# Who normalises the attention weights, and when the convolution's taps run, in a two-layer hybrid kernel

## The chip, the core and the metric

The kernel runs on one core of a Trainium2 chip. The metric is device time in microseconds (us) of one execution. The core has five engines with in-order queues of their own: TensorE (PE; PEld is its weight load), VectorE (DVE), ScalarE (ACT), GpSimd (POOL) and SyncE (SP), which here only issues transfers.

## What is computed

The reference is a two-layer transformer over 512 latent tokens of width 1024, with 256 context tokens. The change touches layer 0 only, its mixer. One input projection feeds two branches, whose outputs are concatenated and multiplied by one output matrix:

```python
def attend(q, k, v):          # q (B,Q,H,QK), k (B,L,H,QK), v (B,L,H,V); 8 heads, 512 queries, 768 keys
    s = jnp.einsum('bqhd,bkhd->bhqk', q, k).astype(jnp.float32) * (QK_DIM ** -0.5)
    p = jax.nn.softmax(s, axis=-1).astype(v.dtype)
    return jnp.einsum('bhqk,bkhd->bqhd', p, v)
...
def conformer_conv(g, w_dw, b_dw, ln_g, ln_b):
    a, b = jnp.split(g, 2, axis=-1)
    z = a * jax.nn.sigmoid(b)
    z = lax.conv_general_dilated(z, w_dw[:, None, :], (1,), padding=[(15, 15)], ...) + b_dw   # 31 taps per channel
    return jax.nn.silu(layer_norm(z, ln_g, ln_b))
```

Queries, keys and values come from low-rank latents with norms and a rotary part. After the mixer, and again in layer 1 (a gated MLP over chunks), a mixture of 32 experts follows, each with its own weights from HBM.

## The kernel before

**The stages of layer 0's mixer**, with the stretch of the profiled execution that they take. Up to some 103 us: modulation, norms, the gated input of the convolution (`z`, 512 channels as four blocks of 128 partitions, 512 positions each). To 145 us: `latent(i)` (L1127), for two context blocks and four latent blocks of 128 tokens, each a product in three passes (`mm3`, the float32 weights split into a high and a low part). To 190 us: the keys and values of six token blocks (L1192) and the first two of the four blocks of queries (`query`, L1174). Then `attend` (L1235): 32 units of one head and one block of 128 queries. Then `Project.run` (L1478), the output projection, first with the attention's output, then with the convolution's.

**A unit of attention.** `scores(u)` (L1241): two products give 128 x 768 scores in PSUM; VectorE takes the maximum of each row (L1249) and scales it (L1250); ScalarE writes the exponentials to SBUF and sums them (L1252); VectorE takes the reciprocal of the sum (L1253) and multiplies the 768 columns by it, SBUF to SBUF (L1254). `values(u - 2)` (L1257), two units later: TensorE transposes the weights in six pieces (L1266), ScalarE copies four of them out of PSUM (L1269) and VectorE two (L1271); for every second unit TensorE multiplies them with the values of two heads (L1280), and the result is split into a high part by ScalarE and a low part by VectorE (`split`, L811). The loop at L1284 runs `scores(u)`, one tick of the queue `q`, `values(u - 2)`, at u of 3 and 11 a block of queries, and one step of `extra`, which computes modulation vectors for later (`ada`, eight 1 MB weight tiles for each of three groups, L826) and fetches.

**The convolution in the background.** `conv_steps` (L978) is a generator. Each of its first 31 steps adds one tap to all four channel blocks. Block 0 is always on VectorE, one instruction a tap (L991, both inputs and the output in SBUF). Block 1 is on VectorE as well in the first `NDVE` = 20 steps. Otherwise a block's tap is a scaling on ScalarE into a temporary (L996, a tile of the ring "w2" of 6) and an addition on GpSimd (L997). Then follow the sum over blocks, three empty steps, the mean, the variance, Sqrt, Silu and the split (L999 to L1029), 12 steps more.

**What sets the order.** `Later` (L40) holds the background work. Every `tick` adds `rate` to a credit, and each whole credit runs one step:

```python
        if self.bg:
            self.credit += self.rate
        while self.bg and self.credit >= 1:
            self.credit -= 1
            if next(self.bg[0], self) is self:
```

The rate is `RATE0` = 0.25 from L1115 on, `RATE1` = 1.0 in `attend`. There are 10 ticks in the latents (one for each context block, two for each latent block), 8 in the keys and first queries and 3 in the flush after them. So 5 steps (ticks 4, 8, 12, 16, 20) are done before the first unit, and one more with every unit. What is left after the loop is drained in the projection, by `conv()` (L1228). The taps' instructions on VectorE and ScalarE are kept in program order (`pin`); most others are placed on their queues by a planner that works out an order beforehand.

Of the kernel before, what the change touches and what calls it, by code (L numbers as in the profile page):

```python
# [12 lines left out]
AF = mybir.ActivationFunctionType  # L13
OP = mybir.AluOpType
# [781 lines left out]
def bank(k, name):  # L796
    return k.psum.tile([P, 512], F32, name=name, tag="ps")


def bank2(k, name):  # L800
    return k.psum.tile([P, 1024], F32, name=name, tag="pd", bufs=2)
# [176 lines left out]
def conv_steps(k, z, acc, ya):  # L978


    nc, pin = k.nc, k.tc.keep_in_program_order
    for m, j in enumerate([15] + [j for j in range(31) if j != 15]):
        lo, hi = max(0, 15 - j), min(512, 527 - j)
        for t in range(4):
            zz, d = z[:, t, lo + j - 15:hi + j - 15], acc[:, t, lo:hi]
            w = k.wdw[:, t, j:j + 1]
            if t == 0 or (t == 1 and m < NDVE):
                if m == 0:
                    pin(nc.vector.tensor_scalar(d, zz, w, k.bdw[:, t:t + 1], op0=OP.mult, op1=OP.add))
                else:  # L990
                    pin(nc.vector.scalar_tensor_tensor(d, zz, w, d, op0=OP.mult, op1=OP.add))  # L991
            elif m == 0:
                pin(nc.scalar.activation(d, zz, AF.Identity, bias=k.bdw[:, t:t + 1], scale=w))
            else:
                tp = k.work.tile([P, 512], F32, name="ctp", tag="w2", bufs=NW2)[:, 0:hi - lo]
                pin(nc.scalar.activation(tp, zz, AF.Copy, scale=w))  # L996
                nc.gpsimd.tensor_tensor(d, d, tp, op=OP.add)  # L997
        yield
# [33 lines left out]
def attention_mixer(k, x, ctx, extra, proj):  # L1032

    nc, q = k.nc, k.q
# [129 lines left out]

    for i in (4, 5, 0, 1, 2, 3):
        latent(i)

    wuk = load_parts(k, [k.w_ukv], 2, 1024, "wuk", nc.gpsimd)
    wuq = [load_parts(k, [k.w_uq[b]], 3, 384, "wuq", nc.gpsimd) for b in range(2)]
# [53 lines left out]
    ya = Parts(k, 4, 512, "yc")  # L1223
    back.append(ya)
    attend(k, qx, kx, kc, vt, y, extra, query, proj)
    q.rate = RATE2

# [7 lines left out]
def attend(k, qx, kx, kc, vt, y, extra, query, proj):  # L1235

    nc, q = k.nc, k.q
    units = [(hp, i, e) for i in range(4) for hp in range(4) for e in range(2)]
    held, PTs = {}, {}

    def scores(u):  # L1241
        hp, i, e = units[u]
        h = 2 * hp + e
        ps = bank2(k, "ps_s")
        a = qx[h // 4][0:QK, h % 4, i * P:(i + 1) * P]
        nc.tensor.matmul(ps[:, 0:512], a, kx[h // 4][0:QK, h % 4], start=True, stop=True)
        nc.tensor.matmul(ps[:, 512:768], a, kc[0:QK, h], start=True, stop=True)
        mx = k.small.tile([P, 4], F32, name="mx4", tag="mx4", bufs=4)
        nc.vector.tensor_reduce(mx[:, 0:1], ps[:, 0:768], axis=AX.X, op=OP.max)  # L1249
        nc.vector.tensor_scalar(mx[:, 1:2], mx[:, 0:1], -SCALE, None, op0=OP.mult)  # L1250
        pr = k.work.tile([P, 768], F32, name="pr", tag="t3", bufs=4)
        nc.scalar.activation(pr, ps[:, 0:768], AF.Exp, bias=mx[:, 1:2], scale=SCALE, accum_out=mx[:, 2:3])  # L1252
        nc.vector.reciprocal(mx[:, 3:4], mx[:, 2:3])  # L1253
        nc.vector.tensor_scalar(pr, pr, mx[:, 3:4], None, op0=OP.mult)  # L1254
        held[u] = pr

    def values(u):  # L1257
        hp, i, e = units[u]
        pr = held.pop(u)
        if e == 0:  # L1260
            PTs[0] = k.work.tile([P, 2, 6, P], F32, name="PT", tag="PT", bufs=2)
        PT = PTs[0]
        for a, b in ((0, 4), (4, 6)):
            pt = bank(k, "ps_pT")
            for c in range(a, b):
                nc.tensor.transpose(pt[:, (c - a) * P:(c - a + 1) * P], pr[:, c * P:(c + 1) * P], k.ident)  # L1266
            src = pt[:, 0:(b - a) * P].rearrange("p (c t) -> p c t", c=b - a)
            if a == 0:
                nc.scalar.copy(PT[:, e, a:b], src)  # L1269
            else:  # L1270
                nc.vector.tensor_copy(PT[:, e, a:b], src)  # L1271
        if e == 0:
            return

        def pv():
            po = bank(k, "ps_pv")
            for c in range(6):
                for e in range(2):
                    v = vt[hp // 2][:, c, 128 * (hp % 2) + 64 * e:128 * (hp % 2) + 64 * e + 64]
                    nc.tensor.matmul(po[64 * e:64 * e + 64, 0:P], v, PT[:, e, c, :], start=(c == 0), stop=(c == 5))  # L1280
            split(k, y(0, hp, i * P, i * P + P), y(1, hp, i * P, i * P + P), po[:, 0:P])
        q.push(YL, pv)

    for u in range(len(units) + 2):  # L1284
        if u < len(units):
            scores(u)
        q.tick()
        if u >= 2:
            values(u - 2)
        if u in QK1:  # L1290
            query(len(QK0) + QK1.index(u), False)
        if u == 26:
            proj.fetch()
        next(extra, None)
    q.flush()
# [296 lines left out]
QK1 = [3, 11]  # L1592
PRE0 = [4, 2, 1, 0]
PRE1 = [0, 0, 0, 0, 0, 2, 2, 0]
NDVE = 20
RATE0, RATE1 = 0.25, 1.0


def body(tc, nc, x, ctx, cc, w_ada, w_ada0, b_ada, norm1, norm2, w_ab, w_glu, w_lat, w_uq, w_ukv, ab_w_out, c_w_in, c_b_in, c_lng, c_lnb, c_wsT,
# [272 lines left out]
```

## Time and profile before

| | |
|---|---|
| median of 3 runs | 1419.5 us (1416.41 to 1420.37) |
| the profiled execution's own time | 1422.08 us |
| its span, first to last instruction | 1420.3 us |
| TensorE busy, share of the span | 1223.8 us, 86% |
| VectorE | 743.0 us, 52% |
| ScalarE | 514.3 us, 36% |
| GpSimd | 288.6 us, 20% |
| mean granted TensorE clock | 0.949 of full speed |

A profile is of one execution. Busy time of an engine is the time in which it worked on an instruction; matmuls are pipelined, and their ends are modelled, so that TensorE's share is not its distance from its peak. An idle engine costs nothing unless another waits for it. The shares are means over stages with different limits, and the stage that the change touches takes about a fifth of the span.

### The profile page before, as it was taken

Reading aid. Unit: us, or ns where it says so; the run is one execution under the profiler, and the core shown is the slowest. Engines: PE = TensorE matmul, PEld = TensorE weight load, DVE = VectorE, ACT = ScalarE, POOL = GpSimd, SP = SyncE. Lnnn points to the kernel's source line nnn. Section 1 sums busy time; section 2 is a strip of 40 time slices with the busy share of each in tenths; the row PEclk is TensorE's granted clock in tenths of the full one; section 3 lists DMA queues with packets and bytes.
Section 4 is the critical chain, followed back from the end, with each engine's and each line's share of the span. In section 5 each row is a group of like instructions: output and inputs, shape, how many; then the busy total and the mean of one; then the engine's idle time right before and its main releaser. Section 6 shows DMA issues by size and latency. Waiting matters only on the chain. (4 is left out here: it accounts for less than half of the span.)

```text
span 1420.3 us, 19799 instructions
## 1 busy us (share of the span) xinstructions
PE 1223.8 (86%) x6894; PEld 793.5 (56%) x6894; DVE 743.0 (52%) x1598; ACT 514.3 (36%) x1235; POOL 288.6 (20%) x270
## 2 busy tenths in 40 slices
PE   5999878899996989989969999999995787777775
PEld 2678654455673444444458898997873333333333
DVE  2334778889567556564684456667346411111116
ACT  3244554476444434333352233335224312211111
POOL 0033455587002011121230001221002100000000
PEclk9999989899997999999989999999997999999998
DMA  9401044726847799989856364453367699988883
GB/s 359 160 29 47 18 155 149 296 72 245 318 157 260 282 365 413 413 347 381 366 179 221 105 231 135 159 172 131 148 237 261 241 365 358 366 342 326 347 325 124
DMA packets 59298, 341.13 MB, mean 240 GB/s; under 512 B 9817, under 2 KB 10073, under 8 KB 24370
## 3 DMA queue, kind: packets, MB, share of 16 engines
q1 hardware_dynamic: 50834, 314.68, 57.1%
q0 software_dynamic: 8224, 23.61, 5.0%
q8 instruction: 106, 1.74, 0.5%
q14 instruction: 134, 1.10, 0.2%
HBM read 321.96 MB, written 21.80 MB: 242 GB/s over the span
## 5 line engine op out<-in xcount | busy, mean ns | idle before, releaser
L357 PE MATMUL mps<-w,xT 128*64 128x512 f32 x1024 | 250.2, 640 | 44.5 <-issue 30.5
L357 PEld LDWEIGHTS mps<-w,xT 128*64 128x64 f32 x1024 | 100.2, 147 | 188.9 <-issue 183.4
L806 PE MATMUL ps_c<-wch,hxh 128*128 128x256 f32 x512 | 147.7, 289 | 2.0 <-ACT hxh L812 2.0
L808 PE MATMUL ps_c<-wch,hxl 128*128 128x256 f32 x512 | 146.0, 286 | 1.5 <-DVE rm_m L98 0.9
L807 PE MATMUL ps_c<-wcl,hxh 128*128 128x256 f32 x512 | 146.2, 286 | 0.0
L363 DVE TENSOR_TENSOR mix<-mix,mps 128x256 f32<-128x256 f32 x32 | 13.5, 421 | 235.0 <-ACT mix L362 235.0
L430 PE MATMUL mps<-w,mix 128*64 128x512 f32 x512 | 116.9, 598 | 8.4 <-ACT mix L371 6.6
L362 ACT ACTIVATE mix<-mps 128x256 f32<-128x256 f32 x32 | 12.3, 384 | 275.1 <-PE mps L357 275.1
L997 POOL TENSOR_TENSOR acc<-acc,ctp 128x497 f32<-128x497 f32 (+14 forms) x71 | 103.1, 1481 | 29.4 <-ACT ctp L996 29.4
L806 PEld LDWEIGHTS ps_c<-wch,hxh 128*128 128x128 f32 x512 | 99.1, 194 | 7.8 <-issue 4.2
L808 PEld LDWEIGHTS ps_c<-wch,hxl 128*128 128x128 f32 x512 | 99.0, 194 | 4.5 <-issue 1.7
L807 PEld LDWEIGHTS ps_c<-wcl,hxh 128*128 128x128 f32 x512 | 99.2, 194 | 4.2 <-issue 3.4
L411 POOL TENSOR_TENSOR X<-X,tmp 128x512 f32<-128x512 f32 x32 | 41.2, 1287 | 203.8 <-ACT tmp L410 180.4
L430 PEld LDWEIGHTS mps<-w,mix 128*64 128x64 f32 x512 | 35.1, 136 | 71.5 <-issue 54.3
L400 PE MATMUL mps<-oy,ooh 128*128 128x512 f32 x272 | 72.7, 408 | 1.7 <-ACTq L729 1.7
L413 DVE TENSOR_TENSOR X<-X,mps 128x512 f32<-128x512 f32 x101 | 64.6, 683 | 5.8 <-PE mps L400 4.9
L806 PE MATMUL ps_o<-woh,yTh 128*128 128x512 f32 x160 | 63.9, 402 | 2.9 <-DVE res L1538 1.7
L807 PE MATMUL ps_o<-wol,yTh 128*128 128x512 f32 x160 | 63.6, 397 | 0.0
L808 PE MATMUL ps_o<-woh,yTl 128*128 128x512 f32 x160 | 62.9, 394 | 0.0
L400 PEld LDWEIGHTS mps<-oy,ooh 128*128 128x128 f32 x272 | 48.5, 189 | 24.9 <-issue 12.1
L812 POOL TENSOR_TENSOR vs<-v,vs 128x512 fp32r<-128x512 f32 x16 | 23.0, 1440 | 182.1 <-ACT vs L812 174.7
L991 DVE SCALAR_TENSOR_TENSOR acc<-z,cl,acc 128x508 f32<-128x508 f32 (+14 forms) x49 | 58.8, 1223 | 0.0
(429 smaller groups left out, 2408.4 us busy)
## 6 DMA issues: line engine op xcount, KB each, us to landing
w<-in_w_gu_dram SPq DMA_DIRECT2D x128, 1024.0 KB
w<-in_w_down_dram SPq DMA_DIRECT2D x64, 1024.0 KB
wada<-in_w_ada_dram SPq DMA_DIRECT2D x48, 1024.0 KB
wc<-in_c_w_in_dram SPq DMA_DIRECT2D x16, 1024.0 KB
wo<-in_c_w_out_dram SPq DMA_DIRECT2D x8, 1024.0 KB
X<-in_x_dram SPq DMA_DIRECT2D x4, 1024.0 KB
wo<-in_ab_w_out_dram SPq DMA_DIRECT2D x4, 1024.0 KB
yd<-zero SPq DMA_DIRECT2D x4, 1024.0 KB
```

The costliest lines, as they stand in the source:

```text
L357: k.nc.tensor.matmul(m.pg[64 * h:64 * h + 64, :], m.xT[:, c, 64 * h:64 * h + 64], st.gu(p, h, c), start=(c == 0), stop=(c == 7))
L363: k.nc.vector.tensor_tensor(m.h, m.sg, m.pg[:, 256:512], op=OP.mult)
L400: k.nc.tensor.matmul(po, self.oh[:, i * P:i * P + P], y[:, 512 * n:512 * n + 512], start=start and y is self.y[0], stop=stop and y is self ...
L411: k.nc.gpsimd.tensor_tensor(X[i][:, c], X[i][:, c], m.tmp, op=OP.add)
L413: k.nc.vector.tensor_tensor(X[i][:, c], X[i][:, c], po, op=OP.add)
L430: nc.tensor.matmul(m.py[n][64 * h:64 * h + 64, :], m.hT[:, f, 64 * h:64 * h + 64], st.dn(p, h, f)[:, 512 * n:512 * n + 512], start=(f == 0 ...
L806: k.nc.tensor.matmul(out, lh, rh, start=start, stop=False)
L807: k.nc.tensor.matmul(out, lh, rl, start=False, stop=False)
L808: k.nc.tensor.matmul(out, ll, rh, start=False, stop=stop)
L812: for i in (k.nc.scalar.copy(hi, src), (eng or k.nc.vector).tensor_tensor(lo, src, hi.bitcast(F32), op=OP.subtract)):
L991: pin(nc.vector.scalar_tensor_tensor(d, zz, w, d, op0=OP.mult, op1=OP.add))
L997: nc.gpsimd.tensor_tensor(d, d, tp, op=OP.add)
```

## The change

The normalisation L1254 leaves VectorE: `normal(u)` does it on ScalarE, as a copy with a scale for each row, issued after the unit's tick and before `values(u - 2)`. In the convolution, block 1 stays on VectorE in all 31 steps, not in 20. The rate is 0.75 while the latents are computed, 0.25 with the keys and first queries (`RATE01`), and 1.0 in the attention loop as before.

```diff
--- before.py
+++ after.py
@@ -984,7 +984,7 @@
         for t in range(4):
             zz, d = z[:, t, lo + j - 15:hi + j - 15], acc[:, t, lo:hi]
             w = k.wdw[:, t, j:j + 1]
-            if t == 0 or (t == 1 and m < NDVE):
+            if t < 2:
                 if m == 0:
                     pin(nc.vector.tensor_scalar(d, zz, w, k.bdw[:, t:t + 1], op0=OP.mult, op1=OP.add))
                 else:
@@ -1164,6 +1164,7 @@
 
     for i in (4, 5, 0, 1, 2, 3):
         latent(i)
+    q.rate = RATE01
 
     wuk = load_parts(k, [k.w_ukv], 2, 1024, "wuk", nc.gpsimd)
     wuq = [load_parts(k, [k.w_uq[b]], 3, 384, "wuq", nc.gpsimd) for b in range(2)]
@@ -1251,12 +1252,15 @@
         pr = k.work.tile([P, 768], F32, name="pr", tag="t3", bufs=4)
         nc.scalar.activation(pr, ps[:, 0:768], AF.Exp, bias=mx[:, 1:2], scale=SCALE, accum_out=mx[:, 2:3])
         nc.vector.reciprocal(mx[:, 3:4], mx[:, 2:3])
-        nc.vector.tensor_scalar(pr, pr, mx[:, 3:4], None, op0=OP.mult)
-        held[u] = pr
+        held[u] = pr, mx
+
+    def normal(u):
+        pr, mx = held[u]
+        nc.scalar.activation(pr, pr, AF.Copy, scale=mx[:, 3:4])
 
     def values(u):
         hp, i, e = units[u]
-        pr = held.pop(u)
+        pr, _ = held.pop(u)
         if e == 0:
             PTs[0] = k.work.tile([P, 2, 6, P], F32, name="PT", tag="PT", bufs=2)
         PT = PTs[0]
@@ -1285,6 +1289,8 @@
         if u < len(units):
             scores(u)
         q.tick()
+        if u < len(units):
+            normal(u)
         if u >= 2:
             values(u - 2)
         if u in QK1:
@@ -1592,8 +1598,7 @@
 QK1 = [3, 11]
 PRE0 = [4, 2, 1, 0]
 PRE1 = [0, 0, 0, 0, 0, 2, 2, 0]
-NDVE = 20
-RATE0, RATE1 = 0.25, 1.0
+RATE0, RATE01, RATE1 = 0.75, 0.25, 1.0
 
 
 def body(tc, nc, x, ctx, cc, w_ada, w_ada0, b_ada, norm1, norm2, w_ab, w_glu, w_lat, w_uq, w_ukv, ab_w_out, c_w_in, c_b_in, c_lng, c_lnb, c_wsT,
```

## Rows read from the trace of the kernel before

**Rows 1.** Windows by stage: length, busy us (instructions) of each engine, TensorE's clock, DMA.

```profile
103.00:145.00 42.00, 38.67 (x253) 36.83 (x252) 17.43 (x50) 16.96 (x53) 17.60 (x31) 1.00 0.15 47
145.00:190.00 45.00, 35.35 (x175) 29.55 (x174) 34.59 (x90) 21.23 (x56) 17.01 (x19) 0.92 0.25 100
190.00:341.00 151.00, 130.06 (x806) 70.44 (x805) 131.14 (x232) 87.34 (x167) 105.51 (x81) 0.91 0.43 159
341.00:366.00 25.00, 23.83 (x182) 15.55 (x183) 19.14 (x38) 12.93 (x26) 9.38 (x8) 1.00 0.92 337
366.00:380.00 14.00, 11.62 (x55) 8.92 (x55) 7.99 (x10) 6.87 (x10) 0.00 (x0) 0.97 1.02 422
```

**Rows 2.** Groups, 190 to 341 us: shapes, count | busy us, mean ns | idle before.

```profile
L991 DVE SCALAR_TENSOR_TENSOR acc<-z,cl,acc 128x508 f32<-128x508 f32 (+14 forms) x42 | 51.9, 1259 | 0.0
L1249 DVE TENSOR_REDUCE mx<-ps_s 128x1 f32<-128x768 f32 x28 | 26.5, 947 | 2.1 <-PE ps_s L1247 2.1
L1254 DVE TENSOR_SCALAR pr<-pr,mx 128x768 f32<-128x768 f32 x27 | 26.5, 981 | 0.5
L1271 DVE COPY PT<-ps_pT 128x256 f32<-128x256 f32 x25 | 10.3, 413 | 8.3 <-PE ps_pT L1266 8.2
L1253 DVE RECIPROCAL mx<-mx 128x1 f32<-128x1 f32 x27 | 4.2, 154 | 4.2 <-ACT pr L1252 4.1
...
L996 ACT ACTIVATE ctp<-z,cl 128x501 f32<-128x501 f32 (+14 forms) x65 | 42.2, 710 | 1.0 <-DVE ada_sb L843 1.0
L1252 ACT ACTIVATE pr<-ps_s,mx 128x768 f32<-128x768 f32 x27 | 24.2, 899 | 25.4 <-DVE mx L1250 23.7 <-PE ps_pT L1266 1.6
...
L997 POOL TENSOR_TENSOR acc<-acc,ctp 128x501 f32<-128x501 f32 (+14 forms) x65 | 94.2, 1480 | 23.1 <-ACT ctp L996 23.1
```

**Rows 3.** Waits from 190 to 341 us: total, times, longest.

```profile
ACT pr L1252 <- DVE mx L1250: 23.7, 13, 5.2
...
PE ps_pT L1266 <- DVE yTl L812: 8.2, 4, 2.8
...
PE ps_pT L1266 <- DVE PT L1271: 5.2, 4, 1.8
```

**Rows 4.** One line's instructions: shortest, median and longest in ns.

```profile
L991 DVE SCALAR_TENSOR_TENSOR acc<-z,cl,acc x49: 677/1206/2770, 131.8 to 337.4; 128x508 f32<-128x508 f32 x4, 128x509 f32<-128x509 f32 x4, 128x510 f32<-128x510 f32 x4, 128x511 f32<-128x511 f32 x4
...
L1254 DVE TENSOR_SCALAR pr<-pr,mx x32: 603/797/1717, 193.9 to 362.0; 128x768 f32<-128x768 f32 x32
...
L997 POOL TENSOR_TENSOR acc<-acc,ctp x71: 1062/1552/2456, 136.8 to 340.2; 128x497 f32<-128x497 f32 x5, 128x498 f32<-128x498 f32 x5, 128x499 f32<-128x499 f32 x5, 128x500 f32<-128x500 f32 x5
```

**Rows 5.** Timeline of TensorE from 340.8 us: start, duration, instructions.

```profile
340.82 1.12 PE L1246 MATMUL ps_s<-kx,qx 96*128 96x512 f32 x2
...
344.57 1.06 PE L826 MATMUL ps_ada<-wada,sc 128*32 128x512 f32 x8
345.57 1.12 PE L1246 MATMUL ps_s<-kx,qx 96*128 96x512 f32 x2
...
346.96 1.02 PE L1006 MATMUL ps_m<-csum,avg 128*128 128x512 f32 x2
347.83 0.82 PE L1266 MATMUL ps_pT<-ct,pr 128*128 128x128 f32 x6
...
349.57 0.70 PE L1246 MATMUL ps_s<-kx,qx 96*128 96x512 f32 x1
```

**Rows 6.** Timeline of GpSimd, 129 to 160 us, and a wait from 103 to 190.

```profile
129.32 4.74 POOL L812 TENSOR_TENSOR wukl<-wuk,wukh 128x1024 fp32r<-128x1024 f32 x2 [4.87 <-ACT wukh L812]
...
146.93 2.94 POOL L812 TENSOR_TENSOR wuql<-wuq,wuqh 128x384 fp32r<-128x384 f32 x3 [1.23 <-ACT wuqh L812]
151.49 0.62 POOL L1207 TENSOR_TENSOR kt<-krr,hrs 128x256 f32<-128x256 f32 x1 [1.62 <-DVE hrs L102]
155.02 3.48 POOL L997 TENSOR_TENSOR acc<-acc,ctp 128x498 f32<-128x498 f32 x2 [2.91 <-ACT ctp L996]
...
PE ps_hd L970 <- POOL kt L1207: 6.5, 3, 3.4
```

**Rows 7.** Timeline of TensorE in the output projection: idle time in brackets.

```profile
378.63 0.50 PE L806 MATMUL ps_o<-woh,ych 128*128 128x512 f32 x1 [2.38 <-ACT ych L812]
```

## The prediction, made before the change was run

> **What bounds the kernel now.** I read the busy times by stage first. The change touches the stretch from the latent projections to the output projection, so only that is cut into stages [rows 1]. Before 145 us TensorE is busy 38.7 of 42 us: the projections are TensorE-bound, and VectorE, ScalarE and GpSimd each work less than half of the time. From 145 to 190 (keys, values, first queries) TensorE drops to 35.4 of 45. From 190 to 341, attention with the convolution's taps woven in, VectorE is busy 131.1 of 151 us, 87%. TensorE shows 130.1, but at a granted clock of 0.91; at full clock that is 130.1 x 0.91 = 118 us. From 341 to 366, with the taps gone, TensorE is busy 23.8 of 25 at clock 1.00.
>
> The groups of 190 to 341 [rows 2] show what fills VectorE: 42 taps 51.9 us, the row maxima 26.5, the normalisation 26.5, the copies of transposed weights 10.3. The reader should see two means: a tap takes 1259 ns and a normalisation 981, though the shortest of each is 677 and 603 [rows 4]. GpSimd's additions likewise take 1480 on average against a shortest 1062. All three read and write SBUF, and as I read it they stretch each other when VectorE and GpSimd meet. The waits [rows 3] show the consequence: the transposes of the weights wait for VectorE (8.2 and 5.2 us), for the small copies that sit behind a pair of taps, and ScalarE's exponentials wait 23.7 us for the scaled maximum. So this stage is set by VectorE's queue and its meeting with GpSimd.
>
> What TensorE alone would need is seen after 341: two units with one product of attention weights and values, from 340.82 to 349.57, less 0.87 for a product of the convolution's mean, so 7.88 us a pair or 3.94 a unit, 1.00 of it modulation work [rows 5]. The stage holds 27 exponentials, so 27 units, in 151 us: 5.6 us each.
>
> **The change, part by part.** *Normalisation moved.* 27 instructions of 0.98 us leave VectorE in this stage, 26.5 us. On ScalarE the same 768 columns are bounded by the exponential over 768 columns, 0.90 us, and, from below, by the 500-column scaling of the taps, 0.71 us [rows 2]; I take 0.90, the same width, so 24 us more for ScalarE. ScalarE waits with it for the reciprocal; behind it on its queue stand the copy of unit u-2's transposes and the next exponential, which TensorE and VectorE wait for. Between exponential and normalisation lie the tap's two scalings, 1.4 us, which should cover the reciprocal. *Half of the convolution on VectorE.* In steps 20 to 30 one channel block goes from ScalarE and GpSimd to VectorE: 11 scalings and 11 additions less, 11 taps more. *Taps earlier.* A step costs one credit. The latents give 10 ticks, the keys and the flush 11. At 0.25 throughout, 5 steps are done when attention begins; at 0.75 and then 0.25 it is 7 in the latents and 3 after them, 10 in all. The steps among the keys stay on the ticks that they had. In the attention loop the taps end with unit 20 instead of 25, and the whole chain behind them (mean, variance, swish) now ends on the tick of unit 32, before the output projection.
>
> Attention stage, VectorE: it had 42 taps and 27 normalisations; it gets 42 taps (21 steps of two) and none, while GpSimd's additions fall from 65 to 42. VectorE falls to 131 - 26.5 = 105 us, and lower if the taps shrink with GpSimd's load. ScalarE: 87.3 + 24 - 23 x 0.71 = 95. GpSimd: 105.5 - 23 x 1.48 = 71. TensorE then leads. Its work lies between 27 x 3.94 = 106 (no query projections in it) and 118; I take 114, above the middle for the projections. No engine reaches 100% in a loop of in-order queues that wait for each other; the leading one had 87% before, and I take the same for TensorE: 114 / 0.87 = 131 us, against 151, so **-20 us**. Bounds: TensorE without a gap at the middle, 112, gives -39; VectorE's queue staying what sets the pace gives about 0.
>
> *Tail.* TensorE waits 2.38 us for the convolution's output in the output projection [rows 7]. With the chain ended inside the loop this goes: **-2.4 us** (0 to -4; next in line is the next weight's split). Its Sqrt and Silu table loads now fall among the last exponentials; if the order puts Sqrt between two of them, two reloads come in, on a ScalarE that is idle 12 of the 25 us there [rows 1].
>
> *Latents and keys.* Five steps come in: 10 taps on VectorE (0.68 to 1.26 us each, 7 to 13 us), 10 scalings on ScalarE (7 us), 10 additions on GpSimd (1.06 to 1.48, 11 to 15). Before 145 they are costed at nothing: TensorE's own 38.7 us covers them, with VectorE at 17.4 and GpSimd at 17.6 of 42 [rows 1]. What is not covered is the last of them, on the last latent's last tick, just ahead of the first keys. GpSimd also splits the key and query weights there (4.74 us for one pair) and multiplies the rotary keys at 151.49, and TensorE already waits 6.5 us for that product [rows 6]. A pair of additions before it costs 2 to 3.5 us. Bounds: 0, if the queue is empty by then, as it was from 149.9, and +5 with a second pair behind; I take **+3**.
>
> No transfer is added. Faster units, at 114 / 0.87 / 27 = 4.9 us or at best 4, ask for the modulation weights sooner: 1 MB in 4 us is 262 GB/s, against the 422 GB/s that the queue moves from 366 to 380 [rows 1]. The expert weights are issued as slots come free, so they move with TensorE.
>
> Sum: -20 - 2.4 + 3 = -19.4. The profiled execution took 1422.1 us (span 1420.3 and 1.8 around it), which gives 1402.7; it lies 2.6 over the median of the runs shown, so the median to expect is **1400 us**.
>
> **Rivals.** *The meeting of VectorE and GpSimd still sets the pace.* Two taps and two additions remain in every one of 21 units, and only the normalisation has gone. For it: the taps' mean of 1259 against 677 is the larger share of the stretch. Against it: GpSimd's additions fall by a third. The units with taps stay at 5.6 us, five of them become units without (5 x (5.6 - 3.94) = 8 us), tail -2.4, keys +3: 1419.5 - 7.4 = 1412. The Trainium skill, "SBUF — State Buffer", Who interferes with whom, gives this mechanism as an exclusive lock that a VectorE instruction with two SBUF inputs and a GpSimd instruction that reads SBUF take in turn. By that rule the taps alone keep the lock busy, and 1412 is the time; the rows bear out the stretch, not that it decides.
>
> *ScalarE's queue becomes the bound (the other side).* Place: the normalisation of unit u, which waits for VectorE's reciprocal. If the order leaves the reciprocal behind the previous step's taps (a pair takes 2.5 us at the mean), ScalarE stands, and the next exponential and the copy behind it with it. Price: 2 us in each of 21 units is 42 us, against the 19.4 of the sum: 1419.5 - 19.4 + 42 = 1442. It decides from 1.0 us a unit on. For it: ScalarE at 95 of 131 us, with VectorE's answer needed in each unit. Against it: the scalings stand between, and before, the reciprocals waited 4.2 us in all for exponentials [rows 2]. The Trainium skill, "ScalarE: Activation LUTs", Rules for kernel authors, speaks against the change outright: multiplications belong on VectorE. By that rule each move loses 0.3 us (0.90 against 0.60), some 10 us; the trace agrees only for the shortest instruction, the mean of 0.98 is above 0.90.
>
> *The early taps delay the keys in full.* All ten additions end up ahead of the weights' splits: 10 x 1.06 = 11 us more on the path, so 1400 + 11 - 3 = 1408.
>
> **How the numbers follow.** My forecast 0.68, the lasting lock 0.15, ScalarE's queue 0.09, the early taps 0.08. Within 0.3%, or 4.3 us, is about what a measurement of this kernel can tell from no change. Faster by more: 0.66 of the forecast, 0.10 of the lock case (1412 lies not far past the line at 1415.2), 0.07 of the early taps, 0.83. Slower by more: ScalarE's queue 0.09 and 0.01 of the lock case, 0.10. The rest is 0.07. The range runs from -38 (TensorE nearly without a gap, 1381) to 1417, which takes in the lock case and the delayed keys; outside are ScalarE's queue and the edges.
>
> **What would show it.** Right: from the first score to the last, some 20 us less; TensorE busy over 85% of the loop with a granted clock nearer 1; VectorE under 85%; the waits of the transposes for VectorE below half; the taps' mean near 1.0 us; no wait for the convolution's output in the projection. Wrong: units with taps still at 5.6 us; ScalarE waiting for the reciprocal by tens of us; a gap before the first keys' transposes of over 5 us.

## The result, and the profile after

The change made the kernel slower: 1426.5 us median (1418.8 to 1435.1, 20 runs) against 1416.5 (1410.4 to 1428.5, 20 runs), a ratio of 1.0066, 95% interval 1.0047 to 1.0084. Forecast were 1400 us, at most 1417. The profiled execution after has a span of 1422.6 us, 2.1 under its median less the 1.8 around it; that of before lies 5.6 over its own. So the two traces differ by only 2.3 us where the medians differ by 10.0: medians say how much, and the traces say where.

The windows ahead of the attention come first, from the first product of the latents to the last one and from there to the first score: two rows of before, then two of after. Then come the 27 units of after from the first score on. The columns are those of [rows 1], and the last row sums the two windows above it.

```profile
101.78:144.58 42.80, 39.47 (x258) 37.66 (x257) 18.12 (x51) 16.92 (x52) 18.40 (x31) 1.00 0.13 42
144.58:188.56 43.98, 34.34 (x172) 29.02 (x171) 33.15 (x86) 21.27 (x56) 17.43 (x20) 0.92 0.27 106
...
100.61:154.33 53.72, 42.56 (x259) 40.40 (x257) 29.32 (x59) 21.43 (x60) 30.06 (x40) 0.94 0.11 36
154.33:204.70 50.37, 36.78 (x172) 30.94 (x172) 37.41 (x88) 22.14 (x58) 19.68 (x21) 0.86 0.22 89
...
204.70:239.70 35.00, 27.34 (x146) 14.53 (x146) 24.16 (x57) 21.52 (x37) 17.82 (x20) 0.90 0.19 66
239.70:340.80 101.10, 92.44 (x640) 51.48 (x638) 81.07 (x153) 75.75 (x137) 65.87 (x47) 1.00 0.62 237
sum 136.10, PE 119.78 PEld 66.01 DVE 105.22 ACT 97.26 POOL 83.69; mean PE 59.89 PEld 33.00 DVE 52.61 ACT 48.63 POOL 41.84
```

The latents take 10.9 us more and the keys and first queries 6.4 more, 17.3 in all. Of this 11.8 us are idle time of TensorE (7.8 in the latents, 4.0 behind them), and 5.5 are the same products at a lower clock (0.94 for 1.00, then 0.86 for 0.92). The first score comes at 204.7 us instead of 188.6. The same 27 units that took 149.2 us before (first exponential 192.7, the 28th 341.9) take 136.1. The gain is there, and it was spent before the attention began.

The rows of the attention's groups in those 136 us, of after, answer to [rows 2] (line numbers are one to five higher; L1259 is the moved normalisation):

```profile
L997 POOL TENSOR_TENSOR acc<-acc,ctp 128x505 f32<-128x505 f32 (+14 forms) x44 | 63.6, 1470 | 25.6 <-ACT ctp L996 25.6
L991 DVE SCALAR_TENSOR_TENSOR acc<-z,cl,acc 128x505 f32<-128x505 f32 (+14 forms) x44 | 49.5, 1158 | 0.0
...
L1259 ACT ACTIVATE pr<-pr,mx 128x768 f32<-128x768 f32 x26 | 24.3, 934 | 4.3 <-DVE mx L1254 4.1
L1253 ACT ACTIVATE pr<-ps_s,mx 128x768 f32<-128x768 f32 x27 | 24.2, 897 | 14.3 <-DVE mx L1251 9.5 <-PE ps_pT L1270 1.9 <-DVE a2c L854 1.7
```

The normalisation on ScalarE takes 0.93 us and waits 4.1 us in all for the reciprocal; the exponentials wait 9.5 us for the scaled maximum, not 23.7 [rows 3].

What TensorE waited for from 100 to 210 us, of after (total, times, longest):

```profile
PE ps_latT L1160 <- DVE lt L1155: 14.5, 5, 4.7
PE ps_hd L970 <- POOL kt L1208: 6.7, 3, 3.6
```

The second row is as before [rows 6]. The first was, in the kernel before:

```profile
PE ps_latT L1160 <- DVE lt L1155: 3.0, 4, 1.6
```

TensorE stands at the transposes of the latents' normalised rows. The timeline of after around the longest of these waits, ScalarE, GpSimd, VectorE and TensorE in turn:

```profile
129.33 0.49 ACT L1140 ACTIVATE jkl<-ps_lat 128x384 bf16<-128x384 f32 x1 [4.35 <-PE ps_lat L808]
129.72 0.19 ACT L1140 ACTIVATION_READ_ACCUMULATOR jkl<-ps_lat 128x1 f32 x1
129.81 0.70 ACT L996 ACTIVATE ctp<-z,cl 128x499 f32<-128x499 f32 x1
130.42 0.28 ACT L97 ACTIVATE rm_y<-lst,eps 128x2 f32<-128x2 f32 x1
...
130.59 2.44 POOL L997 TENSOR_TENSOR acc<-acc,ctp 128x499 f32<-128x499 f32 x2 [3.30 <-ACT ctp L996]
132.99 2.34 POOL L812 TENSOR_TENSOR wukl<-wuk,wukh 128x1024 fp32r<-128x1024 f32 x1
...
130.73 0.17 DVE L99 RECIPROCAL rm_y<-rm_y 128x2 f32<-128x2 f32 x1 [0.61 <-ACT rm_y L97]
130.93 0.93 DVE L100 TENSOR_TENSOR rm_a<-rm_y 128x2 f32<-128x2 f32 x1
131.89 1.17 DVE L101 SCALAR_TENSOR_TENSOR rm_a<-rm_a,rm_m 128x2 f32<-128x2 f32 x1
133.09 2.26 DVE L102 SCALAR_TENSOR_TENSOR lst<-rm_a,rm_y 128x2 f32<-128x2 f32 x1
135.39 1.01 DVE L1155 SCALAR_TENSOR_TENSOR lt<-ps_lat,lst,gains 128x256 f32<-128x256 f32 x2
...
130.93 0.29 PE L808 MATMUL ps_lat<-wih,hxl 128*128 128x288 f32 x1
135.93 1.49 PE L1160 MATMUL ps_latT<-ct,lt 128*128 128x128 f32 x5 [4.71 <-DVE lt L1155]
...
137.77 0.52 PE L807 MATMUL ps_lat<-wil,hxh 128*128 128x384 f32 x1
138.09 0.52 PE L808 MATMUL ps_lat<-wih,hxl 128*128 128x384 f32 x1
...
139.54 0.33 PE L808 MATMUL ps_lat<-wih,hxl 128*128 128x384 f32 x1
```

The same chain in the kernel before, one latent at the same place, ScalarE, VectorE and TensorE:

```profile
127.78 0.19 ACT L1140 ACTIVATION_READ_ACCUMULATOR jkl<-ps_lat 128x1 f32 x1
...
128.54 0.16 DVE L100 TENSOR_TENSOR rm_a<-rm_y 128x2 f32<-128x2 f32 x1
128.73 0.16 DVE L101 SCALAR_TENSOR_TENSOR rm_a<-rm_a,rm_m 128x2 f32<-128x2 f32 x1
128.93 0.16 DVE L102 SCALAR_TENSOR_TENSOR lst<-rm_a,rm_y 128x2 f32<-128x2 f32 x1
129.13 1.01 DVE L1155 SCALAR_TENSOR_TENSOR lt<-ps_lat,lst,gains 128x256 f32<-128x256 f32 x2
...
129.45 0.29 PE L808 MATMUL ps_lat<-wih,hxl 128*128 128x288 f32 x1
...
130.28 0.52 PE L1160 MATMUL ps_latT<-ct,lt 128*128 128x128 f32 x3 [0.18 <-DVE lt L1155]
```

Read from the square: ScalarE's sum is out at 129.91. Behind it stands a tap's scaling, so the root begins at 130.42. That scaling releases GpSimd's addition at 130.59, and while the addition and then a weight split run, VectorE's instructions of two columns take 0.93, 1.17 and 2.26 us instead of 0.16. The normalised rows are done at 136.40, 6.5 us after the square; before, it was 2.2 us (127.97 to 130.14). TensorE's queue holds only 1.3 us of other products (to 131.22) ahead of the transposes, so it stands for 4.7 us. Before, it held 1.8 us (to 129.74), and TensorE waited 0.2. Then, in after, its products of 384 columns follow each other every 0.32 us instead of 0.17: after the idle stretch the granted clock is at the lower of its two levels, 1.2 GHz, until about 139 (0.83 in the mean from 130 to 140).

Two other stretches of after look the same, with waits of 2.5 and 2.4 us. In the last latent's chain, with a wait of 4.5 us, no scaling stands ahead of the root; there two taps stand between the stretched instructions on VectorE:

```profile
156.29 0.72 DVE L991 SCALAR_TENSOR_TENSOR acc<-z,cl,acc 128x502 f32<-128x502 f32 x1
156.93 1.03 DVE L100 TENSOR_TENSOR rm_a<-rm_y 128x2 f32<-128x2 f32 x1
157.89 1.63 DVE L991 SCALAR_TENSOR_TENSOR acc<-z,cl,acc 128x502 f32<-128x502 f32 x1
159.44 0.94 DVE L101 SCALAR_TENSOR_TENSOR rm_a<-rm_a,rm_m 128x2 f32<-128x2 f32 x1
```

### The profile page after: what moved, and what is told of

It is laid out like the page before. It is cut to its first block, busy times and chain, and to the rows that moved or that the text cites. A ratio compares the mean times of both kernels' runs of the same rounds, so it can differ in the third digit from the quotient of the medians.

```text
span 1422.6 us, 19778 instructions
## 1 busy us (share of the span) xinstructions
PE 1222.4 (86%) x6894; PEld 795.7 (56%) x6894; DVE 725.7 (51%) x1577; ACT 534.7 (38%) x1257; POOL 271.9 (19%) x259
## 5 line engine op out<-in xcount | busy, mean ns | idle before, releaser
L997 POOL TENSOR_TENSOR acc<-acc,ctp 128x497 f32<-128x497 f32 (+14 forms) x60 | 83.9, 1423 | 42.1 <-ACT ctp L996 42.1
L413 DVE TENSOR_TENSOR X<-X,mps 128x512 f32<-128x512 f32 x101 | 64.7, 683 | 5.9 <-PE mps L400 5.0
L991 DVE SCALAR_TENSOR_TENSOR acc<-z,cl,acc 128x497 f32<-128x497 f32 (+14 forms) x60 | 63.9, 1096 | 0.0
```

The lines of the kernel that those rows point to most:

```text
L413: k.nc.vector.tensor_tensor(X[i][:, c], X[i][:, c], po, op=OP.add)
```

## The experiments

Each is told by its ratio to the kernel before (1416.5 to 1418.0 us median beside each) and by two distances in its trace: **front**, the first product of the latents to the first score, and **middle**, the first score to the start of the projection's last product with the attention's output (the first of its three passes). Before: front 86.8, middle 232.0. After: 104.1 and 219.8. What lies behind the middle is 994 to 1008 us long in every run, mostly 998 to 1004; the profiles do not say how much of that spread is chance, so differences of a few us are read from the medians.

| kernel | front | middle | median | ratio, 95% interval |
|---|---|---|---|---|
| after | 104.1 | 219.8 | 1426.5 | 1.0066 (1.0047 to 1.0084) |
| before, second profile | 86.8 | 229.5 | one run | |
| late taps | 83.1 | 223.2 | 1410.5 | 0.9961 (0.9942 to 0.9981) |
| early taps alone | 104.2 | 230.9 | 1437.4 | 1.0141 (1.0104 to 1.0178) |
| normalisation alone | 86.8 | 234.6 | 1428.6 | 1.0080 (1.0052 to 1.0107) |
| block on VectorE alone | 86.8 | 236.6 | 1423.2 | 1.0040 (1.0013 to 1.0068) |
| early steps all on VectorE | 90.0 | 224.9 | 1417.1 | 0.9984 (0.9956 to 1.0012) |
| no early additions | 90.0 | 223.6 | 1413.9 | 0.9975 (0.9945 to 1.0005) |
| no early scalings | 86.0 | 224.1 | 1410.6 | 0.9938 (0.9905 to 0.9972) |
| no taps in latents | 76.3 | 236.4 | 1414.5 | 0.9974 (0.9951 to 0.9997) |
| steps moved | 97.7 | 224.2 | 1423.2 | 1.0031 (1.0010 to 1.0051) |
| steps moved, late | 87.7 | 222.8 | 1410.9 | 0.9955 (0.9931 to 0.9979) |
| transposes later | 93.9 | 226.2 | 1419.5 | 0.9987 (0.9956 to 1.0019) |
| transposes later, late taps | 90.1 | 224.4 | 1416.8 | 0.9992 (0.9963 to 1.0022) |
| half rate | 94.9 | 219.4 | 1417.0 | 1.0008 (0.9987 to 1.0029) |
| no taps in the loop | 86.8 | 193.0 | 1383.2 | 0.9756 (0.9721 to 0.9791) |
| normalisation, early mean | 86.7 | 236.9 | 1423.9 | 1.0056 (1.0028 to 1.0084) |
| none, then faster | 76.3 | 241.6 | 1420.1 | 1.0009 (0.9983 to 1.0034) |
| late, then faster | 86.8 | 241.6 | 1435.3 | 1.0121 (1.0084 to 1.0157) |

### The change taken apart

**Late taps**, the changed kernel with the rate of the kernel before:

```diff
-RATE0, RATE01, RATE1 = 0.75, 0.25, 1.0
+RATE0, RATE01, RATE1 = 0.25, 0.25, 1.0
```

> Theory E (the early taps cost): the last latent matmul comes at 144.6 us again instead of 154.3, the first score near 189 instead of 205, and the attention keeps most of its gain (first to last exponential 155.7 us against 166.9; with more taps left for it perhaps 158 to 160). The time is 8 to 12 us below the kernel before, 1405 to 1409 against 1416.5. Rival S (the normalisation on ScalarE and the block on VectorE are what costs, through what they do to the attention and to the stages behind it): the attention's 11 us are given back behind it whatever the latents do, and the time stays within 4 us of 1426, or at best at 1416.

Measured: 1410.5 us, 0.39% under the kernel before and a little above what was expected; the last latent product at 142.9, the first score at 183.2, first to last exponential 158.6. Theory E holds, and rival S falls: from this kernel to the changed one only the rate differs, and it costs 16.0 us of medians.

**Early taps alone**, the kernel before with the rates 0.75 and 0.25:

> Theory E: the last latent matmul at about 154, the first score at about 204, as in the changed kernel; the attention has five steps less to carry and gives back some of it (its last five units with taps become units without, 1.6 us each at the most: 0 to 8 us). The time is 6 to 17 us above the kernel before, 1423 to 1433. Rival S: TensorE covers the early taps, the latents end within 4 us of 144.6, and the time is 1409 to 1417.

Measured: 1437.4, 20 us above the kernel before, more than expected. The front is 104.2, to 0.1 us that of the changed kernel, and the middle gives back nothing clear of the scatter (230.9, for 232.0 and 229.5 in the two profiles of before).

**Normalisation alone** and **block on VectorE alone** (rates as before). The edit is that of the first, against after; the second is the kernel before with this line the other way round:

```diff
-            if t < 2:
+            if t == 0 or (t == 1 and m < NDVE):
```

> Theory E: the latents as in the kernel before; of the attention's 11 us this part carries most, since it alone takes work off VectorE (26.5 us): first to last exponential 156 to 161 us, the time 6 to 10 us below the kernel before. Rival S: 24 us more on ScalarE cost what VectorE gains: first to last exponential 164 us or more, the time within 3 us of the kernel before or above it.

> Theory E: the latents as in the kernel before; VectorE, which sets the pace of the attention, gets 11 taps more and keeps its normalisation, while GpSimd loses 11 additions: first to last exponential 165 to 172 us, the time within 4 us of the kernel before. Rival S: the block on VectorE is what hurts, the time 5 to 10 us above the kernel before.

Measured: 1428.6 and 1423.2. Theory E is wrong on both times; S has both times, but is wrong on the attention of the first. Both are slower than the kernel before, and together (late taps) they are faster: neither part has a price of its own. The first has the shortest attention of all with its taps in the loop (first to last exponential 153.9 us) and loses it behind. TensorE's timeline in its projection:

```profile
365.59 3.63 PE L1537 MATMUL ps_l<-wr,shc 128*128 128x36 f32 x16 [3.89 <-DMA wr<-in_w_r_dram]
369.03 2.05 PE L1019 MATMUL ps_v<-csq,avg 128*128 128x512 f32 x2
379.37 0.79 PE L806 MATMUL ps_o<-woh,ych 128*128 128x512 f32 x1 [8.29 <-ACT ych L812]
```

The variance's product stands on TensorE behind one that waits for its weights, and the projection then waits 8.3 us for the convolution. In the second, VectorE carries two taps and a normalisation in every unit: units 20 to 26 take 6.1 us each, 5.2 before.

**Normalisation, early mean**, to try that order:

```diff
-NY = 3
+NY = 0
```

> The normalisation alone, with the mean over channels taken three ticks earlier (NY 0 for 3). Theory T (its attention is the shortest of all, and what it loses behind it is an order: the product for the variance stands on TensorE behind one that waits 3.9 us for its weights, at 365.6, and the projection then stands 8.3 us for the convolution's output): the variance is formed before the end of the attention, the wait for the convolution's output falls below 3 us, and the time is 1405 to 1415 against 1428.6. Rival D (the loads behind the attention are the bound, at 410 GB/s from 360 to 380, whatever the order): the wait moves to a load, and the time stays at 1422 or more.

Measured: 1423.9, 5 us less than without, which the two intervals do not separate, and still slower than before. Neither theory holds, though the time is in D's range. The wait left the projection and came back in the loop, on GpSimd's sums:

```profile
334.71 2.08 PE L1006 MATMUL ps_m<-csum,avg 128*128 128x512 f32 x2 [5.64 <-POOL csum L1002]
```

With three channel blocks' additions left to GpSimd in the last steps, the convolution is late for a faster attention, wherever its chain enters TensorE's queue. That is what the half on VectorE is for: late taps differ from the normalisation alone by this part only, wait 1.3 us for `ych` instead of 8.3, and take 1410.5 us instead of 1428.6.

### What the early steps do to the latents

**No early additions** and **no early scalings**, in the steps 1 to 6:

```diff
-                nc.gpsimd.tensor_tensor(d, d, tp, op=OP.add)
+                if m >= 7:
+                    nc.gpsimd.tensor_tensor(d, d, tp, op=OP.add)
```

```diff
+            elif 0 < m < 7:
+                nc.gpsimd.tensor_tensor(d, d, zz, op=OP.add)
             elif m == 0:
```

> The changed kernel, leaving out the twelve additions of the six early steps on GpSimd (two channel blocks lack six taps); the scalings stay. Theory G: the short instructions at 0.16 to 0.20 us except beside the split of the key weights, last latent matmul at 143 to 148, first score at 186 to 195, the time 1408 to 1415. Theory A: the last latent matmul stays at 151 or later and the first score at 200 or later.

> The changed kernel, leaving out the twelve scalings of the six early steps on ScalarE; GpSimd adds the unscaled input in their place, so its additions stay. Theory G: the short instructions stay stretched, last latent matmul at 151 or later, first score at 200 or later, the time 1421 to 1429. Theory A: the root follows the squares at once, last latent matmul at 147 or earlier, first score at 195 or earlier.

Measured: the front falls by 14.1 us without the additions and by 18.1 without the scalings. Each theory's own run bears it out, and each is refuted, as it stood, by the other's: without the additions the scalings are all there, without the scalings the additions are, and either way most of the loss is gone. GpSimd's and VectorE's timeline without the scalings (L993 is the addition there) shows why:

```profile
111.00 8.85 POOL L993 TENSOR_TENSOR acc<-acc,z 128x497 f32<-128x497 f32 x7 [1.20 <-ACT acc L995]
...
123.45 4.52 POOL L993 TENSOR_TENSOR acc<-acc,z 128x502 f32<-128x502 f32 x3
...
129.82 0.16 DVE L100 TENSOR_TENSOR rm_a<-rm_y 128x2 f32<-128x2 f32 x1
130.01 0.16 DVE L101 SCALAR_TENSOR_TENSOR rm_a<-rm_a,rm_m 128x2 f32<-128x2 f32 x1
130.21 0.16 DVE L102 SCALAR_TENSOR_TENSOR lst<-rm_a,rm_y 128x2 f32<-128x2 f32 x1
```

Free of the scalings, the additions run ahead, during the products, and from the second latent block on are over when the short instructions come. It is mostly the meeting that costs: the scalings, pinned behind the second square, time the additions to fall on the chain. TensorE waits 2.5 us for the rows there, 5.7 without additions, 14.5 in the changed kernel.

**Early steps all on VectorE**, no scaling and no addition ahead of the keys:

```diff
-            if t < 2:
+            if t < 2 or 0 < m < 7:
```

> The changed kernel with its six early steps wholly on VectorE: four taps a step, no scaling on ScalarE and no addition on GpSimd before the keys. Theory G (the early steps cost because GpSimd's additions stretch VectorE's short instructions between the squares and the transposes, 0.16 us each to 0.9 to 2.3): the short instructions are back at 0.16 to 0.20, the last latent matmul comes at 143 to 147 us instead of 154, the first score at 186 to 195 instead of 205, and the time is 1405 to 1414. Theory A (they cost because two scalings, 1.3 us, stand on ScalarE between the squares and the root): the same, since the scalings go too. Rival V (any tap that comes early costs, because VectorE's queue is in order and a tap of 0.7 us stands ahead of the short instructions): twice as many taps, so the latents end at 154 or later and the time is 1426 or more.

Measured: front 90.0, first score at 190.5 as expected, last latent product at 148.8 and time at 1417.1, both just outside. Rival V falls on every number: 24 early taps on VectorE cost less than 12 there and 12 additions on GpSimd. But what it names does occur: four taps (2.67 us) stand ahead of one latent's short instructions, and TensorE waits 4.6 us there.

**Steps moved**, all work kept; and the same with rate 0.25:

```diff
                     rope(k, krr[:, i:i + 1], kr[:, i:i + 1], krt, i, 1)
-            else:
-                q.tick()
+                    q.tick()
...
-        q.tick()
+        with k.tc.issue_after(root.ins):
+            q.tick()
```

> The changed kernel with all its work, two things moved: the step between a latent's two products is issued ahead of the second product instead of behind its square, and the step at a latent's end behind the root. Theory C (from the two runs before: neither the scalings nor the additions cost by themselves; the scalings, pinned behind the second square, release GpSimd's additions just as VectorE's short instructions run, and both arrive late at the transposes): the root follows its square at once, the short instructions are mostly back at 0.16 to 0.20 us, TensorE waits under 7 us for the latents' normalised rows (14.5 in the changed kernel), the last latent matmul comes at 143 to 148 and the first score at 186 to 196; the time is 1405 to 1414. Rival V (early taps cost wherever they stand, since TensorE's cover is too thin): last latent matmul 150 or later, first score 199 or later, the time 1419 or more.

> The same move with the rate of the kernel before, 0.25, in the latents. Theory C: there is little left to mend with two steps in the latents (TensorE waited 2.2 us there): the time is within 4 us of the 1410.5 of the run with late taps. If it is above the run with the moved early taps by more than 3 us, early taps pay once they don't collide; if below it, they are worth nothing even then.

Measured: 1423.2 and 1410.9. The wait for the rows falls from 14.5 to 8.9 us and the front by 6.4, less than expected; the time is only 3 us better. The root now follows its square at once, in every latent. But GpSimd's weight split, pushed back by the moved additions, meets the chain of the third latent, as GpSimd's and VectorE's timeline there shows (lines one higher):

```profile
135.82 2.47 POOL L998 TENSOR_TENSOR acc<-acc,ctp 128x500 f32<-128x500 f32 x2
138.26 4.73 POOL L813 TENSOR_TENSOR wukl<-wuk,wukh 128x1024 fp32r<-128x1024 f32 x2
...
140.81 2.19 DVE L100 TENSOR_TENSOR rm_a<-rm_y 128x2 f32<-128x2 f32 x1
143.04 1.00 DVE L101 SCALAR_TENSOR_TENSOR rm_a<-rm_a,rm_m 128x2 f32<-128x2 f32 x1
```

So theory C names a mechanism, and the remedy was half of one: a weight split does for the collision as well as an addition. From the second latent on, a tap also stands just ahead of `lt` on VectorE, and rival V's numbers are met or nearly so here (last latent product at 153.2, first score at 198.8, the time above 1419): taps in the chain cost as well. How the loss divides between the two was not separated. At the old rate the moved kernel takes 1410.9 us (1410.5 unmoved), 12 less than with the early taps, so these are worth nothing even moved.

**Transposes later**, with early and with late taps:

```diff
-LL0 = 2
+LL0 = 3
```

> The changed kernel with the transposes of the latents' rows due one tick later (LL0 3 for 2), so that TensorE has half a latent's products more in its queue ahead of them. Theory C: the chain on VectorE is as late as before, but TensorE's wait for it falls from 14.5 us to under 6, and the clock stays up; last latent matmul 143 to 149, first score 188 to 198, the time 1408 to 1418, as far as the keys don't wait for the later transposes in their turn. If the place in TensorE's queue doesn't matter, the waits stay above 10 us and the time within 4 us of 1426.

> The kernel with late taps and the transposes of the latents' rows one tick later. In the kernel with early taps this move took 11 us off the first score. With two steps in the latents TensorE waits only 2.2 us for the rows: theory C gives -2 to +2 us against the 1410.5 of late taps, 1408 to 1413; a gain of over 4 us would say that the latents lose by something else than the steps.

Measured: 1419.5 (front 93.9, wait 7.3 us) and 1416.8. With early taps more products in TensorE's queue ahead of the transposes take back 10 us of the front, though the short instructions are still stretched; the time is 1.5 over what was expected. With late taps the move loses 6 us, not 0, and theory C missed that: it is no gain by itself, it buys cover where cover is short.

**No taps in latents** and **half rate**:

```diff
+RATE0, RATE01, RATE1 = 0.0, 0.25, 1.0
...
+RATE0, RATE01, RATE1 = 0.5, 0.25, 1.0
```

> The changed kernel with no step in the latents at all (rate 0 there), two fewer than the kernel before had. If each early step costs the latents some 2.7 us (16 us between the runs with rate 0.75 and 0.25, for five to six steps), the last latent matmul comes 2 to 5 us earlier than with rate 0.25 (at 139 to 142), the attention gets two to three steps more at 1 to 1.6 us each, and the time is 1405 to 1411, at or a little under the 1410.5 of rate 0.25. If the first steps cost nothing and only a number beyond them does, the latents end at 142 to 144 as with rate 0.25 and the time is 1411 to 1415.

> The changed kernel with rate 0.5 in the latents: five steps in place of seven (0.75) or two (0.25). Theory C: the cost follows the collisions, some 2.5 to 4 us for each step that falls between a square and its root or beside the weights' split; the latents end at 146 to 151, first score 190 to 200, the time 1414 to 1421. If only the last steps, in front of the keys, cost: first score within 3 us of the 183 to 188 of rate 0.25 and the time at 1408 to 1413.

Measured: fronts of 76.3, 83.1, 94.9 and 104.1 us for 0, 2, 5 and 7 steps in the latents. With those among the keys, 2, 5, 7 and 10 steps are issued ahead of the attention, so 27.8 us go with eight steps, 3.5 each. Of the 27.8, 12.7 lie up to the last latent product and 15.1 behind it, among the keys and first queries. Half rate came out as theory C expected. The first two steps in the latents are not free: kernels with two have fronts of 83.1 to 87.7. Yet without any the time is 1414.5, where the second reading put it, since the steps come back in the loop and the convolution ends late: TensorE's longest wait there from 330 to 430 us is

```profile
PE ps_o L806 <- ACT ych L812: 8.4, 1, 8.4
```

### What the taps cost in the attention

**No taps in the loop**, 26 of 31 left out with late taps:

```diff
+        if m >= 5:
+            yield
+            continue
```

> The kernel with late taps, leaving out 26 of the 31 taps: the ticks of the attention loop carry none, what follows the taps stays. It shows how much of the attention the taps hold. Theory Q (the 5.6 us a unit of the prediction is a mean over two kinds of unit: the two in which a query block is projected take 11 to 16 us, the others with taps 4.5 to 4.7): the two long units stay at 8 to 11.5 us, the others fall to 3.9 to 4.1, the first exponential to the last takes 133 to 140 us instead of 158.6, the time is 1385 to 1395. By the prediction's reading (every unit with taps loses 5.6 - 3.94): 122 us or less, the time 1370 to 1376.

Measured: 1383.2, first to last exponential 132.3 us, just below theory Q's range and far from the other, and nearer to Q in the time; but the two long units fall to 6.5 us, so the taps had lengthened those as well, and Q was wrong on that. The 26 steps cost the loop 158.6 - 132.3 = 26.3 us, 1.0 each. The windows of the first 27 units:

```profile
187.30:222.30 35.00, 31.02 (x185) 17.50 (x185) 18.42 (x54) 20.18 (x34) 8.11 (x12) 0.90 0.32 117
222.30:301.90 79.60, 79.60 (x602) 48.12 (x598) 41.38 (x111) 51.23 (x93) 8.38 (x9) 1.00 0.80 273
```

**None, then faster** and **late, then faster**, 1.25 steps a tick in the loop with rate 0 and 0.25 in the latents:

```diff
+RATE0, RATE01, RATE1 = 0.0, 0.25, 1.25
...
+RATE0, RATE01, RATE1 = 0.25, 0.25, 1.25
```

> The changed kernel with no step in the latents and 1.25 steps a tick in the attention loop in place of 1. By the runs so far a step costs 4 us ahead of the attention (first product of the latents to first score 76.3 us at rate 0, 104.1 at 0.75, seven steps) and 1 us in the loop (26.3 us for 26 steps); what the kernel without steps in the latents lost was the end of the convolution, 8.4 us of waiting in the projection. Theory P (place sets the price): with the chain ended inside the loop that wait falls below 3 us, the first score stays at 76 to 80 us from the first product, and the time is 1402 to 1410, the shortest of all. Rival F (the loop's price rises with the rate: three steps in two units instead of two): the loop gets longer by what the wait gave, the time is 1412 to 1418.

> The same faster rate in the loop with rate 0.25 in the latents. The convolution's output was in time there already (1.3 us of waiting), so there is little to gain: 1407 to 1414 by theory P, against 1410.5 at rate 1; 1415 or more by rival F.

Measured: 1420.1 and 1435.3. Theory P falls, rival F has the direction but half the size: the wait for the convolution is gone, and the loop takes 15 to 18 us longer (first to last exponential 177.8 for 162.6, 176.7 for 158.6). The 1.0 us of a step in the loop is a price at one step a unit.

**Before again**, for a second profile:

> The kernel before once more, for a second profile of the same program: how much of a difference between two profiles is scatter. The profile shown has a span 5.6 us over its median. Where the scatter lies in the clock granted behind the projection, the first score comes within 1.5 us of 188.6 and the end of the projection within 2 us of 420.6; where it is spread, they differ by up to 5 us.

Measured: a span of 1418.1; front 86.8 both times, to 0.1 us; middle 229.5 for 232.0; behind it 999.3 for 999.7. So the scatter between these two profiles lies in the middle. The front has scatter too: of eight profiles with the same order of VectorE's, ScalarE's and GpSimd's instructions ahead of the attention, seven have a front of 86.7 to 86.8, and late taps has 83.1, with a granted clock of 1.00 from the last latent product to the first score where the others had 0.92 to 0.96. The early steps thus cost the front 17 to 21 us.

**The best version** is late taps: the first two parts of the change at the old rate, 0.39% (0.19 to 0.58) under the kernel before.

## Why the prediction was wrong

**Latents and keys: the step that failed.** The prediction put "Before 145 they are costed at nothing: TensorE's own 38.7 us covers them" and took +3 for what is not covered. The runs show +17.3 (front 104.1 for 86.8): +10.9 in the latents, where nothing was taken, and +6.4 behind them, where 3 was. The forecast of the last step was near in idle time (+4.0 us, of which 3.7 at the last latent's rows), not in the lower clock. The prediction read a stage's busy shares, VectorE at 17.4 and GpSimd at 17.6 of 42 us [rows 1], as room. The room is not where the chain is: square, root, five short instructions and two scalings of rows, 2.2 us from the square's end to TensorE's transposes, with 1.8 us of other products to cover them in the latent shown, and 1.3 after. What lengthens that chain past its cover TensorE waits for, and after most of these waits it pays once more at the lower clock. The prediction did name the last latent's additions and priced them by their own length; it did not ask which instructions they would run beside. That the early steps cost is shown by the rate alone (late taps); that most of it is the meeting of scalings and additions with the chain, by leaving out either.

**Attention: right in mechanism, off in size.** TensorE's share was forecast at 87% and is 88% (119.8 of 136.1 us); VectorE's at 105 us and is 105.2; ScalarE's at 95 and is 97.3; GpSimd's was put at 71 and is 83.7, as its work beside the additions grew from some 11 us in the loop to 20. What was mis-sized is TensorE's work: 114 us were taken, 119.8 measured. With no tap in the loop the same 27 units take 114.6 us, TensorE busy 110.6 of them with 787 products in the trace; after, 786 are busy 119.8. So the 114 was near the floor, and with taps TensorE is busy longer over the same work. Of the gain, 9.3 us are TensorE's busy time (129.1 in the 27 units before), with a mean granted clock of 0.91 before and 0.97 after, and 3.8 are idle time. The 27 units gained 149.2 - 136.1 = 13.1 us, not 20, and from the first score to the end of the projection 12.2 remain, 9.7 against the second profile of before. The 1400 also started from a median of 1419.5 in three runs; over 20 it is 1416.5.

**Taps and additions.** The taps' mean fell from 1259 to 1158 ns, not to 1000, the additions' from 1480 to 1470. The stretch of the two engines does not fade with a third fewer additions. That bears out half of the first rival: they go on meeting, but in the loop TensorE leads all the same.

**Tail: right, and replaced.** The 2.38 us for the convolution's output are gone [rows 7]. In its place, what TensorE waits for from 340 to 430 us, of after:

```profile
PE ps_l L114 <- ACT h2T L112: 2.6, 4, 0.9
PE ps_o L806 <- ACT woh L812: 1.2, 1, 1.2
```

The projection's products with the attention's output span 65.2 us (359.3 to 424.5), before 64.7 (355.9 to 420.6): nothing was gained. What was said to be next in line, a weight's split, is 1.2 us of it.

**The rivals.** ScalarE's queue did not become the bound: 4.1 us of waiting for the reciprocal, not 42. The third rival (early taps, 0.08) had the place and the sign of the loss on the keys, with a price of 11 us and the wrong mechanism: it let additions stand ahead of the weights' splits, and TensorE waited for no split key or query weight from 100 to 210 us. No case of the prediction had a loss in the latents above its gain in the attention.

The Trainium skill, "SBUF — State Buffer", Who interferes with whom, says that a VectorE instruction with two inputs in SBUF contends with a GpSimd instruction that reads SBUF, and one with a single input outside the two-port modes does not. The trace agrees: beside the additions the reciprocal, with one input, takes 0.17 us as ever, and the three instructions with two inputs take 0.93 to 2.26. The prediction drew on this rule for the attention, where instructions are long, and not for the latents, where it decides.

## What to carry to other kernels

An idle share of a stage is no cover for work that is put into it. Cover is what the waiting engine has in its queue between the release of a chain and the instruction that needs its end; look at that distance (here 1.8 us against a chain of 2.2, and no room for more) before anything is put beside the chain, and try more distance (the transposes one tick later took back 10 us). Work taken off a busy stage has a price in each place: here a step cost 1 us in the attention at one step a unit and some 3.5 us ahead of it. Moving five steps earlier lengthened the front by 17 to 21 us and shortened the middle by 3, and a gain of 6.5 us became a loss of 10. Parts of a change can be losses one by one and a gain together; test the parts, then the sums.

## What the runs showed of the hardware

VectorE's shortest instructions with two inputs in SBUF, two columns wide and 0.16 us long, became 0.93 to 2.26 us in the chain shown, beside GpSimd's additions (1.06 us of 500 columns at the shortest) and splits (2.3 us of 1024 columns): each seems to wait out a whole instruction of GpSimd. So the stretch in proportion is up to 14-fold for them, where a tap's mean of 1.16 is 1.7 times its shortest, 0.68. The scaling of two columns at the head of the chain, with one input, was mostly 0.17 us, but 1.12 and 1.48 in one latent each of two runs (no early scalings, early steps all on VectorE), beside an addition and a split. That it is one GpSimd instruction that is waited out is read from the lengths and was not tried by itself. And after three of TensorE's four waits in the latents of after (4.7, 2.4 and 4.5 us) the granted clock was at 1.2 GHz for some 3.4 us: products of 384 columns started 0.32 us apart instead of 0.17, so that a wait cost more than its length. After the other, of 2.5 us, the clock stayed at 2.4 GHz and the products at 0.17.
